# Two thirds of the tokens get all column chunks beside their GLA; attention's gates and output projections come in small pieces behind the heads

## The chip, the cores and the metric

One core of one Trainium2 chip. The metric is the device time of one launch in microseconds (us); lower is better. TensorE (PE) runs the matmuls and its weight loads (PEld), VectorE (DVE), ScalarE (ACT) and GpSimd (POOL) the rest; SyncE (SP) issues nearly all DMAs.

## What is computed

Two layers of a trunk over 256 context and 2048 latent tokens, 1024 wide, f32. A layer norms and modulates its input, projects it to columns for four mixers and their gates, mixes, and projects back:

```python
h = rms_norm(x, norm_w) * (1 + scale) + shift          # scale, shift, gate = ada(c)
p = split_proj(h @ w_in)                               # 12 chunks of 256 columns and a_lr
a = gla_mixer(...)       # A: gated linear attention, forward and backward over the tokens
b = fourier_mix(...)     # B: FFT over tokens and channels
c = swa_mixer(...)       # C: window attention, 4 heads, 2 key heads, sink logits, rope on q and k
d = na_mixer(...)        # D: 2-D neighbourhood attention, 4 heads, with a relative bias
y = concat([a * silu(a_g), b * silu(b_g), c * silu(c_g), d * silu(d_g)]) @ w_out
x = x + gate * y
```

Context tokens see context alone; latent tokens see both. Layer 1 needs no output for the context.

## The kernel before

**Tokens.** Nine subs of 256 tokens: sub 0 is the context, 1 to 8 the latents. Three groups: T1 = subs 0 to 2, T2 = 3 to 5, T3 = 6 to 8. The activations of a sub lie in SBUF as a pair of high and low f32r parts (`hh`, `hl`, tags of the pool `hp` with 3 buffers each, so one group at a time). Weights come in blocks of 256 columns, 1 MB in four DMAs, and are split in the same way (`load_w`, L204: ScalarE casts, VectorE and GpSimd subtract in turn; `whi`, `wlo` with 2 buffers). A product is three matmuls for each of 8 blocks of the contraction (`mm3`, L216). One chunk of one sub is 2 x 24 = 48 matmuls into one PSUM tile (`ps`, or `pso` in the output projection; pool `pp`, 2 buffers), called a block below.

**Chunks.** `project` (L277) ends a block by its kind: `cq`, `ckv`, `dk`, `dq` are normed (`normrope`, L367; cq and ckv with rope), transposed and stored; the gates `ag`, `bg`, `cg`, `dg` become silu by ScalarE and VectorE and are stored in `scr_g`; the others are stored as they are.

**Order.** The program is written in one sequence; a planner then orders each engine's instructions by its own model of times: whatever has its inputs and a free buffer, first by its place in the written sequence. `high_priority` moves what stands under it to the front of that order. Each engine then runs its list strictly in order.

**A layer** (`trunk`, L1198). For T1 and T2: `first_chunks` (L1157) norms h and projects av, lr, aqk, and stores h in DRAM (`scr_h`, L261); `mix_a` (L1167) loads GLA's inputs, then writes the chunks given as `between` (T1: bv, ckv, dk, dv; T2 those and dq), then `gla_fast` for each sub, then the ada blocks that it is given (`ada_block`, L158: VectorE reductions over weights from DRAM). In layer 0, ada(0, [1]) goes with T1 and ada(1, [0]) with T2. T3 has its kv chunks behind its GLA, then the guard, backward scan (`gla_bwd`) and FFT (`fnet`), then cq and dq. Layer 1 runs layer 0's output projection of T2 (`out_proj(0, [3])`, `[4, 5]`) behind T1's GLA.

**Attention** (`attention`, L1181; `pipeline`, L876). A list of items, one per head and query tile. The front of item i (L822) puts scores into the one PSUM tile `pse` (L830), reduces them with bias and sink on VectorE (L836, negative minimum kept in `am`) and takes the exponential on ScalarE (L844), the reciprocal of its sum on VectorE (L847). Behind items i-2 and i-3 stand the transposes (`ppt`, L862, and of the reciprocals, L866), their copies, the products with v (`py`, L922) and the output (L925). A neighbourhood head loads its bias (L1012, one buffer for each of two alternating heads, in three of four column groups). Phases as integers are neighbourhood row groups (16 items each), lists are window tiles (4 items each), None is the context's rows (8 items): 144 items in layer 0, 128 in layer 1; 64 in each are neighbourhood items over latents.

Between phases stand steps written as whole: `gate(T)` projects four gates of a group; `redo` (L1238) reloads a group's h from `scr_h` (`reload_h`, L264: load, cast, subtract) and projects cq (and dq); `out_proj` (L1088) loads y and g, multiplies (L1083, in place in y, one buffer), splits (`prep_mix`, L1073), then runs 4 blocks a sub, adding to x (L1107). In layer 0, T1's output projection stands behind all heads. All steps read in `ph` (L1247 to L1252).

Of the kernel before, what the change touches and what calls it, by code (L numbers as in the profile page):

```python
# [18 lines left out]
KB = 8  # L19
# [18 lines left out]
class Kern:  # L38
# [205 lines left out]
    def prep_h(self, L, s, save, xs=None):  # L244
# [4 lines left out]
        for t in range(2):  # L249
# [10 lines left out]
            if save:  # L260
                nc.sync.dma_start(self.sh[s][:, :, c], x)  # L261
        return hh, hl

    def reload_h(self, s):  # L264
        nc = self.nc
        hh = self.hp.tile([128, KB, SUB], F32R, tag="hh", name="hh2")
        hl = self.hp.tile([128, KB, SUB], F32R, tag="hl", name="hl2")
        for t in range(2):
            c = slice(t * 128, t * 128 + 128)
            x = self.xp.tile([128, KB, 128], F32, tag="xa", name="x2", bufs=3)  # L270
            nc.sync.dma_start(x, self.sh[s][:, :, c])
            nc.scalar.copy(hh[:, :, c], x)
            (nc.gpsimd if t else nc.vector).tensor_tensor(out=hl[:, :, c], in0=x, in1=hh[:, :, c], op=ALU.subtract)
        return hh, hl
# [798 lines left out]
    def prep_mix(self, L, s):  # L1073
        nc = self.nc
        hh = self.hp.tile([128, KB, SUB], F32R, tag="hh", name="mh")
        hl = self.hp.tile([128, KB, SUB], F32R, tag="hl", name="ml")
        for t in range(2):
            c = slice(t * 128, t * 128 + 128)
# [5 lines left out]
            nc.scalar.copy(hh[:, :, c], y)  # L1084
            (nc.gpsimd if t else nc.vector).tensor_tensor(out=hl[:, :, c], in0=y, in1=hh[:, :, c], op=ALU.subtract)  # L1085
        return hh, hl

    def out_proj(self, L, subs):  # L1088
        nc, a = self.nc, self.a
        with self.tc.high_priority():  # L1090
            mix = {s: self.prep_mix(L, s) for s in subs}
        ws = {}
        for j, s in self.order(range(4), subs):
            if j not in ws:
                with self.tc.high_priority():
                    ws[j] = self.load_w(a["w_out"][L, j])
            wh, wl = ws[j]
            st = 1 if s == 0 else 0
            hh, hl = mix[s]
            ps = self.pp.tile([128, 2, SUB], F32, tag="p", name="pso")  # L1100
            for b in range(2):
                c = slice(b * 128, b * 128 + 128)
                self.mm3(ps[:, b], lambda k: wh[:, k, c], lambda k: wl[:, k, c], lambda k: hh[:, k], lambda k: hl[:, k])
            x = self.ev.tile([128, 2, SUB], F32, tag="sq", name="xo")
            nc.sync.dma_start(x, self.xsrc[L][s][:, 2 * j:2 * j + 2])
            for b in range(2):
                nc.vector.scalar_tensor_tensor(out=x[:, b], in0=ps[:, b], scalar=self.mod[L, "gm"][:, 2 * j + b, st:st + 1], in1=x[:, b], op0=ALU.mult, op1=ALU.add)  # L1107
            nc.sync.dma_start(self.xdst[L][s][:, 2 * j:2 * j + 2], x)


    def scratch(self, L):
# [8 lines left out]
        self.sh = sc("h", [128, KB, SUB])  # L1120
# [36 lines left out]
    def first_chunks(self, L, subs, names, save=True, xs={}):  # L1157
        h = {}
        w = {nm: self.chunk_w(L, nm) for nm in names}
        for s in subs:  # L1160
            with self.tc.high_priority():
                h[s] = self.prep_h(L, s, save and not (L == 1 and s == 0), xs.get(s))
# [18 lines left out]
    def attention(self, L, *phases):  # L1181


        with self.tc.tile_pool(name=f"at{L}", bufs=2) as p:
            items, self.bias = [], {}
# [197 lines left out]
```

## Time and profile before

| what | us |
|---|---|
| median of 3 runs | 2922.6 (2921.6 to 2927.07) |
| the profiled execution | 2924.73 |
| its span, first to last instruction | 2922.9 |
| PE busy | 2702.4 |
| DVE busy | 1619.6 |
| ACT busy | 1066.4 |
| POOL busy | 865.5 |

The span is of one profiled execution, and the sums are made against that execution's time. PEclk is the clock granted to TensorE as a share of 2.4 GHz, a mean over a stretch in which it stands at 2.4 or at 1.2 GHz. Matmuls follow each other in a pipeline, so the mean duration of one is longer than its distance to the next. A wait line says which instruction's engine stood idle and what ended that.

### The profile page before, as it was taken

What the parts mean: (1) busy time and instruction counts of PE and PEld (TensorE: products, weight loads), DVE (VectorE), ACT (ScalarE), POOL (GpSimd) and SP (SyncE); (2) the same over time, 40 slices, a digit from 0 to 9 for tenths busy, and PEclk for the clock granted to TensorE, in tenths of its full rate; (3) what the DMA queues carried; (4) which work ended last, traced back from release to release, by engine and by line L of the source; (5) the groups of instructions that cost most, each with busy time, mean ns of one, the idle gap of its engine ahead of it and who ended that gap; (6) DMA issues with size and microseconds to landing.
All of it is one profiled execution on the core that took longest, in us unless ns stands there. A gap on an engine that the chain in (4) does not pass through costs nothing. (4 is left out here: it accounts for less than half of the span.)

```text
span 2922.9 us, 55816 instructions
## 1 busy us (share of the span) xinstructions
PE 2702.4 (92%) x21206; PEld 2404.3 (82%) x21206; DVE 1619.6 (55%) x3741; ACT 1066.4 (36%) x2344; POOL 865.5 (30%) x922
## 2 busy tenths in 40 slices
PE   5989879988999999999969899999889999999999
PEld 5989869977888778887869799889878888878789
DVE  7564774557465545645483554464583656455544
ACT  3343323323344434344224323334232544444332
POOL 3142322334231213212133333332362413121223
PEclk9999979999999999999979899999999999999999
DMA  8644544255765365453453565342465754556545
GB/s 286 203 123 148 183 127 129 87 165 161 188 175 155 119 176 159 135 169 119 138 184 125 177 199 157 100 129 87 128 184 165 207 150 138 156 159 192 154 140 187
DMA packets 476682, 458.01 MB, mean 157 GB/s; under 512 B 54763, under 2 KB 355565, under 8 KB 476013
## 3 DMA queue, kind: packets, MB, share of 16 engines
q1 hardware_dynamic: 472782, 440.66, 49.7%
q0 software_dynamic: 3616, 13.64, 1.9%
q8 instruction: 170, 2.79, 0.4%
q14 instruction: 114, 0.93, 0.1%
HBM read 339.56 MB, written 114.60 MB: 155 GB/s over the span
## 5 line engine op out<-in xcount | busy, mean ns | idle before, releaser
L220 PE MATMUL ps<-whi,hh 128*128 128x256 f32 x1968 | 588.6, 299 | 40.1 <-DVE nsq L376 21.7
L222 PE MATMUL ps<-whi,hl 128*128 128x256 f32 x1968 | 584.3, 297 | 8.7 <-DVE hl L259 8.5
L221 PE MATMUL ps<-wlo,hh 128*128 128x256 f32 x1968 | 582.6, 296 | 6.4 <-PEq L639 6.4
L213 POOL TENSOR_TENSOR wlo<-wraw,whi 128x512 fp32r<-128x512 f32 x208 | 304.8, 1478 | 580.0 <-ACT whi L212 520.7
L220 PEld LDWEIGHTS ps<-whi,hh 128*128 128x128 f32 x1968 | 394.1, 200 | 50.1 <-DVE nsq L376 20.8
L222 PEld LDWEIGHTS ps<-whi,hl 128*128 128x128 f32 x1968 | 393.7, 200 | 17.2 <-DVE hl L259 12.0
L221 PEld LDWEIGHTS ps<-wlo,hh 128*128 128x128 f32 x1968 | 394.7, 201 | 12.3 <-issue 9.2
L220 PE MATMUL ps<-hh,whi 128*128 128x256 f32 x1376 | 399.5, 290 | 1.9 <-DVE nsq L376 1.9
L222 PE MATMUL ps<-hh,wlo 128*128 128x256 f32 x1376 | 399.9, 291 | 0.0
L221 PE MATMUL ps<-hl,whi 128*128 128x256 f32 x1376 | 396.9, 288 | 0.0
L844 ACT ACTIVATE S<-S,am 128x641 f32<-128x641 f32 (+5 forms) x272 | 226.2, 832 | 358.9 <-DVE am L836 345.4
L220 PE MATMUL pso<-mh,whi 128*128 128x256 f32 x1088 | 318.3, 293 | 1.3 <-DVE xo L1107 1.3
L221 PE MATMUL pso<-ml,whi 128*128 128x256 f32 x1088 | 318.4, 293 | 0.0
L222 PE MATMUL pso<-mh,wlo 128*128 128x256 f32 x1088 | 317.3, 292 | 0.0
L212 ACT CAST whi<-wraw 128x512 fp32r<-128x512 f32 x416 | 230.5, 618 | 142.6 <-PE ps L221 43.2
L191 POOL TENSOR_TENSOR rs<-ms,mhalf 128x8 f32<-128x8 f32 (+2 forms) x140 | 174.2, 1246 | 351.1 <-DVE ms L189 339.9
L222 PEld LDWEIGHTS ps<-hh,wlo 128*128 128x128 f32 x1376 | 263.6, 192 | 11.3 <-issue 10.9
L213 DVE TENSOR_TENSOR wlo<-wraw,whi 128x512 fp32r<-128x512 f32 x208 | 200.7, 972 | 130.3 <-ACT whi L212 118.0
L220 PEld LDWEIGHTS ps<-hh,whi 128*128 128x128 f32 x1376 | 263.8, 192 | 10.1 <-issue 6.5
L221 PEld LDWEIGHTS ps<-hl,whi 128*128 128x128 f32 x1376 | 263.6, 192 | 8.3 <-issue 8.2
L830 PE MATMUL pse<-kst,q 64*128 64x256 f32 (+2 forms) x1184 | 245.2, 458 | 18.0 <-DVE am L836 15.6
L862 PE MATMUL ppt<-idn,S 128*128 128x128 f32 x1360 | 243.6, 284 | 12.9 <-DVE pt L872 4.9
(203 smaller groups left out, 4860.4 us busy)
## 6 DMA issues: line engine op xcount, KB each, us to landing
wraw<-w_in SPq DMA_DIRECT2D x288, 256.0 KB
wraw<-w_out SPq DMA_DIRECT2D x128, 256.0 KB
adaw<-ada_w SPq DMA_DIRECT2D x82, 256.0 KB
scr_g<-ev SPq DMA_DIRECT2D x68, 256.0 KB
g<-scr_g SPq DMA_DIRECT2D x34, 512.0 KB
y<-scr_y SPq DMA_DIRECT2D x34, 512.0 KB
bias<-nbias SPq DMA_DIRECT2D x48, 256.0 KB
scr_h<-x SPq DMA_DIRECT2D x22, 512.0 KB
```

What stands on the lines that cost most here:

```text
L191: nc.gpsimd.tensor_tensor(out=rs, in0=ms, in1=self.mhalf.to_broadcast([128, n]), op=ALU.pow)
L212: nc.scalar.copy(hi[:, k], raw)
L213: (nc.gpsimd if i % 4 else nc.vector).tensor_tensor(out=lo[:, k], in0=raw, in1=hi[:, k], op=ALU.subtract)
L220: nc.tensor.matmul(out, ah(k), bh(k), start=(k == 0), stop=False)
L221: nc.tensor.matmul(out, ah(k), bl(k), start=False, stop=False)
L222: nc.tensor.matmul(out, al(k), bh(k), start=False, stop=(k == KB - 1))
L830: nc.tensor.matmul(p[:, lo:hi], q[r], k, start=True, stop=True, tile_position=(64 * o, 0))
L844: nc.scalar.activation(out=S[:, 0:w], in_=S[:, 0:w], func=AF.Exp, scale=-1.0, bias=m[:, 0:1], accum_out=m[:, 1:2])
L862: nc.tensor.transpose(p[:, i], S[:, (c0 + i) * 128:(c0 + i + 1) * 128], self.idn)
```

## The change

- T1 and T2 get all their chunks as `between` of `mix_a`: kv, then cq, dq and the four gates (`rest`). h is no longer stored or reloaded; `reload_h` and `redo` are gone.
- In layer 0, ada(1, [0]) moves from T2's `mix_a` to T3's.
- Attention gets its side work in pieces, each behind a given item, where it was whole steps between phases. In layer 0: T3's 12 gate blocks behind items 4 to 54; T3's output projection from item 57, its six half loads two items apart, then 12 blocks to item 102; T1's from item 105, half loads one item apart, then 12 blocks to item 142. In layer 1: gates 4 to 54, T3 from 57 to 87, T1 (two subs) from 89 to 126, and after attention `out_proj` of [3, 4] and [5].
- `prep_mix` writes the product into g (3 buffers) in place of y (1 buffer); each half's product stands one step behind its load, and in attention it is pinned behind the VectorE instruction written before it.
- A piece asks for its own weight block and the next.

```diff
-    def reload_h(self, s):
...
-    def prep_mix(self, L, s):
...
-            nc.vector.tensor_tensor(out=y, in0=y, in1=g, op=ALU.mult)
...
+    def prep_mix(self, L, subs, late=False):
...
+        def product(s, c):
+            g, y = got.pop(0)
+            hh, hl = mix[s]
+            ins = nc.vector.tensor_tensor(out=g, in0=y, in1=g, op=ALU.mult)
+            if late:
+                self.tc.keep_in_program_order(ins)
+            nc.scalar.copy(hh[:, :, c], g)
+            (nc.gpsimd if c.start else nc.vector).tensor_tensor(out=hl[:, :, c], in0=g, in1=hh[:, :, c], op=ALU.subtract)
+        halves = [(s, slice(t * 128, t * 128 + 128)) for s in subs for t in range(2)]
+
+        def step(k):
+            if k > 0:
+                product(*halves[k - 1])
+            if k < len(halves):
+                load(*halves[k])
...
+    def pieces(self, order, load, run):
+
+        blocks = list(dict.fromkeys(j for j, _ in order))
+        ws = {}
+
+        def piece(j, s):
+            for x in blocks[blocks.index(j):][:2]:
+                if x not in ws:
+                    with self.tc.high_priority():
+                        ws[x] = load(x)
+            run(j, s, ws[j])
+        return [lambda j=j, s=s: piece(j, s) for j, s in order]
...
+            def give(lo, hi, fs):
+                for k, f in enumerate(fs):
+                    behind.setdefault(lo + k * (hi - lo) // max(len(fs) - 1, 1), []).append(f)
+
+            def out(lo, step, hi, subs):
+                made = []
+                n = 2 * len(subs)
+
+                def prep(k):
+                    if k == 0:
+                        mix, steps = self.prep_mix(L, subs, True)
+                        made.extend((steps, self.out_pieces(L, subs, mix)))
+                    made[0][k]()
+                give(lo, lo + step * n, [lambda k=k: prep(k) for k in range(n + 1)])
+                give(lo + step * n + 1, hi, [lambda k=k: made[1][k]() for k in range(4 * len(subs))])
...
-            self.mix_a(L, T1, (0, [1]) if L == 0 else (1, [1]), lambda: self.chunks(L, T1, kv, h))
+            qs = ["dq", "cq"]
+
+            def rest(subs, h):
+
+                self.chunks(L, subs, kv + qs + gates[:2], h)
+                self.chunks(L, subs, gates[2:], h)
+            self.mix_a(L, T1, (L, [1]), lambda: rest(T1, h))
...
-            self.mix_a(L, T2, (1, [0]) if L == 0 else None, lambda: self.chunks(L, T2, kv + ["dq"], h))
-            h = self.first_chunks(L, T3, first, False)
-            self.mix_a(L, T3)
+            self.mix_a(L, T2, None, lambda: rest(T2, h))
+            h = self.first_chunks(L, T3, first)
+            self.mix_a(L, T3, (1, [0]) if L == 0 else None)
             self.chunks(L, T3, kv, h)
...
+            gate = self.pieces(self.order(gates, T3), lambda nm: self.chunk_w(L, nm), lambda nm, s, w: self.project(L, nm, s, h[s], w))
             if L == 0:
-                ph += [b(self.out_proj, L, T3), b(redo, T2, ["cq"]), 1, [4, 5, 6, 7, 8, 9], gate(T2), f(self.out_proj, L, T1)]
+                self.attention(L, [3, 2, [10, 11, 12, 13, 14, 15], 0, [-2, -1, 0, 1, 2, 3], None, 1, [4, 5, 6, 7, 8, 9]],
+                               [(4, 54, gate), (57, 2, 102, T3), (105, 1, 142, T1)])
             else:
...
+                self.attention(L, [3, 2, [10, 11, 12, 13, 14, 15], 0, [0, 1, 2, 3], 1, [4, 5], [6, 7], [8, 9]],
+                               [(4, 54, gate), (57, 2, 87, T3), (89, 2, 126, T1)])
+                self.out_proj(L, [3, 4])
+                self.out_proj(L, [5])
```

## Rows read from the trace of the kernel before

**Rows 1.** Page, part 1: engine busy us (share) xinstructions.

```profile
PE 2702.4 (92%) x21206; PEld 2404.3 (82%) x21206; DVE 1619.6 (55%) x3741; ACT 1066.4 (36%) x2344; POOL 865.5 (30%) x922
```

**Rows 2.** Busy by stretch: length, engines busy (instructions), PEclk, DMA share, GB/s.

```profile
63.00:305.00 242.00, 228.93 (x1790) 219.21 (x1790) 139.85 (x317) 86.50 (x179) 73.13 (x65) 0.99 0.52 163
305.00:451.00 146.00, 121.65 (x790) 108.56 (x791) 110.30 (x273) 47.74 (x113) 45.61 (x35) 0.84 0.47 142
451.00:600.00 149.00, 146.50 (x1158) 139.28 (x1157) 70.61 (x171) 57.87 (x131) 42.02 (x38) 0.99 0.36 114
757.00:1457.00 700.00, 680.82 (x5757) 574.46 (x5756) 365.95 (x863) 279.75 (x644) 158.40 (x236) 0.99 0.52 153
1457.00:1550.00 93.00, 60.54 (x400) 57.22 (x399) 67.13 (x146) 22.69 (x37) 32.86 (x29) 0.80 0.62 191
1550.00:1750.00 200.00, 184.42 (x1396) 177.51 (x1395) 98.11 (x188) 71.59 (x144) 70.58 (x58) 0.94 0.53 165
1750.00:1920.00 170.00, 159.78 (x1202) 151.95 (x1201) 82.63 (x180) 63.66 (x137) 58.51 (x49) 0.93 0.40 121
2237.00:2816.00 579.00, 566.32 (x4833) 466.94 (x4835) 317.08 (x741) 252.10 (x575) 144.82 (x212) 0.99 0.58 166
```

**Rows 3.** Busy by stretch: 40 us of output projection alone, layer 1's end.

```profile
2870.00:2910.00 40.00, 40.00 (x335) 40.00 (x335) 6.40 (x15) 1.00 0.67 212
```

**Rows 4.** Busy by stretch, tile ps alone: PE first, both attentions.

```profile
757.00:1457.00 700.00, 256.44 (x1803) 227.47 (x1801) 25.96 (x38) 22.47 (x38) 0.99 0.52 153
2237.00:2816.00 579.00, 214.50 (x1488) 187.24 (x1488) 21.65 (x32) 18.45 (x31) 0.99 0.58 166
```

**Rows 5.** Busy by stretch, tile pso alone: PE first, both attentions.

```profile
757.00:1457.00 700.00, 165.11 (x1148) 145.65 (x1149) 20.14 (x46) 0.99 0.52 153
2237.00:2816.00 579.00, 110.28 (x744) 95.28 (x744) 13.06 (x30) 0.99 0.58 166
```

**Rows 6.** Waits, 305 to 451: who <- for whom: us, times, longest.

```profile
PE ps L220 <- DVE nsq L376: 14.0, 4, 9.4
...
DVE adaj L167 <- DMA adaw<-ada_w: 17.3, 6, 5.0
```

**Rows 7.** Groups, 305 to 451: VectorE's ada reductions | busy, mean ns | idle.

```profile
L167 DVE CUSTOM_DVE_ANT_0 adaj<-adaw,csb,ada 128x512 f32<-128x512 f32 x32 | 27.1, 846 | 6.0 <-DMA adaw<-ada_w 5.6
L167 DVE CUSTOM_DVE_ANT_0 adaj<-adaw,csb 128x512 f32<-128x512 f32 x32 | 22.6, 705 | 12.1 <-DMA adaw<-ada_w 11.7
```

**Rows 8.** Timeline, TensorE at 1040: start us, us, engine, line, op, tiles.

```profile
1040.30 0.91 PE L830 MATMUL pse<-kst,q 64*128 64x384 f32 x4
1041.14 0.44 PE L862 MATMUL ppt<-idn,S 128*128 128x128 f32 x2
1041.41 0.27 PE L866 MATMUL ppt<-idn,rd 128*128 128x128 f32 x1
1041.52 0.49 PE L862 MATMUL ppt<-idn,S 128*128 128x128 f32 x3
1042.25 0.91 PE L830 MATMUL pse<-kst,q 64*128 64x384 f32 x4 [0.23 <-DVE am L836]
```

**Rows 9.** Timeline, VectorE at 1041, the same heads.

```profile
1041.36 0.82 DVE L836 CUSTOM_DVE_ANT_0 S<-pse,bias 128x640 f32<-128x640 f32 x1
...
1043.18 0.16 DVE L847 RECIPROCAL rc<-am 128x1 f32<-128x1 f32 x1 [0.52 <-ACT S L844]
```

**Rows 10.** Timeline at 769: one bias load and the reduction behind it.

```profile
769.22 0.55 SPq L1012 DMA_DIRECT2D bias<-nbias  x1
...
774.14 0.82 DVE L836 CUSTOM_DVE_ANT_0 S<-pse,bias 128x640 f32<-128x640 f32 x1 [0.71 <-DMA bias<-nbias]
```

**Rows 11.** Waits, 757 to 1457, of TensorE and of VectorE.

```profile
PE pse L830 <- DVE am L836: 10.8, 7, 5.1
...
DVE y L1083 <- DMA y<-scr_y: 34.5, 10, 5.4
```

**Rows 12.** Page, part 6: DMA issues xcount, KB each.

```profile
scr_h<-x SPq DMA_DIRECT2D x22, 512.0 KB
```

More of the change, by code (lines that the diff above doesn't have):

```diff
@@ L1070, in na_ctx_rows, with load @@
                 for a in ((hp, t, i) for hp in range(2) for t in range(2) for i in range(2))]
-    def prep_mix(self, L, s):
+    def prep_mix(self, L, subs, late=False):
         nc = self.nc
[L1075 to L1078, printed above, removed]
+        mix = {s: [self.hp.tile([128, KB, SUB], F32R, tag=n, name=m) for n, m in (("hh", "mh"), ("hl", "ml"))] for s in subs}
+        got = []
+        def load(s, c):
             g = self.xp.tile([128, KB, 128], F32, tag="xa", name="g", bufs=3)
@@ L1092, in out_proj @@
-        ws = {}
[L1093 to L1108, printed above, removed]
+            for f in steps:
+                f()
@@ new lines, in out_proj, with out_pieces @@
+        for f in self.out_pieces(L, subs, mix):
+            f()
+    def out_pieces(self, L, subs, mix):
+        return self.pieces(self.order(range(4), subs), lambda j: self.load_w(self.a["w_out"][L, j]), lambda j, s, w: self.out_block(L, j, s, mix[s], w))
+    def pieces(self, order, load, run):
+        blocks = list(dict.fromkeys(j for j, _ in order))
+        ws = {}
+        def piece(j, s):
[5 more added lines that the diff above has]
+        return [lambda j=j, s=s: piece(j, s) for j, s in order]
@@ L1161, in first_chunks @@
             with self.tc.high_priority():
-                h[s] = self.prep_h(L, s, save and not (L == 1 and s == 0), xs.get(s))
+                h[s] = self.prep_h(L, s, xs.get(s))
             for nm in names:
@@ L1179, in mix_b, with attention @@
             self.fnet(L, p, ctx)
-    def attention(self, L, *phases):
+    def attention(self, L, phases, spread):
         with self.tc.tile_pool(name=f"at{L}", bufs=2) as p:
-            items, self.bias = [], {}
+            items, self.bias, behind = [], {}, {}
+            def give(lo, hi, fs):
[11 more added lines that the diff above has]
+                give(lo + step * n + 1, hi, [lambda k=k: made[1][k]() for k in range(4 * len(subs))])
+            for sp in spread:
+                (out if len(sp) == 4 else give)(*sp)
             for ph in phases:
@@ L1190, in attention, with wrap, last @@
                     items += self.na(L, p, ph)
-                elif isinstance(ph, tuple):
-                    run, nop = lambda f=ph[1]: f(), lambda *r: None
-                    items.append((None, run, nop) if ph[0] == "before" else (None, nop, lambda r, x, f=ph[1]: x == 2 and f()))
-                elif ph:
+                else:
                     items += self.swa(L, p, ph)
-            self.pipeline(items)
+            def wrap(i, item):
+                def last(r, x):
+                    item[2](r, x)
+                    if x == 2:
+                        for f in behind.pop(i, []):
+                            f()
+                return item[0], item[1], last
+            self.pipeline([wrap(i, it) for i, it in enumerate(items)])
+            assert not behind
     def trunk(self):
```

56 lines of the change are left out of this document (21 added, 35 removed).

## The prediction

> **What bounds the kernel now.** I read the page's first part, then the busy time by stage, then waits and timelines inside the stages. TensorE is busy 2702.4 us of 2922.9, VectorE 1619.6, ScalarE and GpSimd less [rows 1]: the end is set by TensorE's work and by its holes. That work does not change here, since the change only moves blocks. So the question is what the holes cost, stage by stage.
>
> I price a stage as its idle time (length less PE busy) plus what the lower clock costs, (1 - PEclk) x PE busy: a mean of 0.84 is 2.4 GHz for about two thirds of a stage and 1.2 GHz for the rest. From the rows by stage [rows 2]: layer 0, tokens T1 (63 to 305 us) 13.1 + 2.3 = 15; T2 (305 to 451) 24.4 + 19.5 = 44; T3's GLA (451 to 600) 4; attention (757 to 1457) 19.2 + 6.8 = 26. Boundary to layer 1 (1457 to 1550) 32.5 + 12.1 = 45. Layer 1: T1 with layer 0's late output projections (1550 to 1750) 27; T2 (1750 to 1920) 21; attention (2237 to 2816) 12.7 + 5.7 = 18. Together 200 us of 2922.9. The holes sit beside the GLA and at the boundary; attention, 1279 us long, has few. A change that takes work out of attention and lays it beside GLA moves filler from a place where it is used to a place where it lacks.
>
> **The change part by part.**
>
> *Size of what moves.* A dense stretch of output projection issues 335 matmuls in 40 us, 0.119 us each [rows 3]; a block (one chunk, one sub) is 48 of them, 5.73 us. In layer 0, T1's cq, dq and gates (6 chunks x 3 subs) and T2's cq and gates (5 x 3) go from attention to GLA: 33 blocks, 189 us. In layer 1 sub 0 needs none: 12 + 15 = 27 blocks, 155 us. By itself this adds to one stage what it takes from another: 0.
>
> *T2 of layer 0.* The 44 us has one named cause beside the lack of filler: TensorE waited 14.0 us, once 9.4, for a projection's PSUM that VectorE had not read [rows 6], while VectorE worked through ada(1, [0]): 64 reductions, 27.1 + 22.6 = 49.7 us [rows 7], and stood 17.3 us more waiting for their weights [rows 6]. The change puts 15 more blocks there (cq and the four gates; dq was there) and takes the ada away. T1's stage, which had 12 column blocks beside its GLA, loses 15 of 242 us, 6%. At that rate T2 loses 9 to 10: **gain 34**, bounds 0 (GLA queues behind the chunks and runs bare afterwards) and 40.
>
> *The ada in T3.* The same 49.7 us now lies with T3's GLA, ahead of T3's remaining chunks and of the backward scan and FFT. VectorE is busy 70.6 of 149 us there [rows 2]; with 49.7 and 17.3 of waiting it comes to 138 of 149. PE has filler there, yet its PSUM is freed by the same VectorE. Bounds: 4 as now, 44 as in T2. I take 20, nearer to now since the stage has filler throughout: **cost 16**.
>
> With the blocks go their weights and ends: 11 chunk loads a layer, 44 DMAs of 256 KB on SP's queue behind GLA's small loads and stores, their casts on ScalarE, half the subtractions each on VectorE and GpSimd, and the norm and rope of cq and dq. T2's stage has room for its part: without the ada's 49.7, VectorE is busy 61 of 146 us, ScalarE 48, GpSimd 46, and DMA is at 0.47 [rows 2]. Cost 0; without that room it would be D's price, below.
>
> *Layer 1, T1 and T2.* T1 keeps ada(1, [1]), T2 has none, before and after; 27 blocks arrive. At T1's 6% they would lose 13 and 11 in place of 27 and 21: **gain 24**, bounds 0 and 40.
>
> *Boundary.* Last out-projection of layer 0, store, load, norm, projection of layer 1: a chain. T1's projections now run among the last heads instead of alone behind them, so the first two subs end a little before the attention's drain. **Gain 5**, bounds -5 and 17 (three blocks' cover).
>
> *Attention with less filler.* Layer 0's attention holds 1803 ps and 1148 pso matmuls [rows 4, 5], 2951 x 0.119 = 352 us; the other 680.8 - 352 = 328 us are the 144 heads' own, 2.28 us each. Layer 1: 2232 matmuls, 266 us, leaving 300 us for 128 heads, 2.34 us. So a head had 20.5 filler matmuls (17.4 in layer 1). 33 x 48 = 1584 of the 1803 leave: 219 + 1148 = 1367, 9.5 a head. (45 blocks are traced for this stretch, 2160 matmuls, and only 1803 lie in it: 357 ran before the first head although they stand behind 56 heads in the program. The order is greedy, filler is pulled as far ahead as its inputs allow.) In layer 1, 1488 - 1296 = 192 and 20 output blocks, 960: 9.0 a head.
>
> If pieces are pulled ahead and each head that has any takes as many as now, 1367 / 20.5 = 67 heads are fed and 77 are bare; in layer 1, 66 fed and 62 bare: 139. Price of a bare head: two stand in the trace. From one score matmul to the next 1.95 us, transposes alone between them [rows 8]; VectorE's round from reduction over ScalarE's exponential to reciprocal 1.98 us [rows 9]. Both are under the 2.3 us of a head's own work, so a bare head of the window attention idles little: 0 to 0.3, I take 0.15. A neighbourhood head needs its bias in one buffer for every second head: issue at 769.22, reduction started at 774.14, having waited for it [rows 10], so 4.9 + 0.8 + 0.1 of reduction = 5.8 to 5.9 for two heads, 2.95 each, 0.64 over its own work. 128 of the 272 heads are of that kind: 65 x 0.64 + 74 x 0.15 = 53 us. Other bound: evenly spread, 3.4 us of PE work a head is over 2.95 and nothing is lost.
>
> *The product y x g.* Now VectorE waited 34.5 us for y in layer 0's attention, and PE 10.8 us for reductions behind it [rows 11]. The pinned product comes two heads after its load (4.6 us bare), which covers most of waits of 3.45 us on average; for T1 of layer 0 one head after, six times, where VectorE still stands some 1.2 us (3.45 - 2.3) with the next heads' reductions and copies queued behind it. y is free after the product instead of after the cast and the subtraction. I take 5 us on PE, bounds 0 and 15.
>
> Attention after: 53 + 5 + 12.5 of clock as now = 70 against 44 now: **cost 26**, bounds a gain of 20 (nothing bare, no waits) and a loss of 100 (below).
>
> *Removed.* 22 stores of h and 22 loads of 512 KB each [rows 12], with cast and subtraction of every load. ScalarE is busy 279.8 and VectorE 366.0 of attention's 700 us, DMA at 0.52 [rows 2], so they cost TensorE nothing and give back nothing; if that cover were gone they would be a gain. *The tail of layer 1*: out_proj of subs 3 to 5 keeps 12 blocks, 69 us, to cover their own loads; 0. Weights are loaded as often as before.
>
> **Sum.** 34 - 16 + 24 + 5 - 26 = 21 us. The profiled execution took 2924.7 us (span 2922.9, the rest around it), 0.1% over the median of 2922.6. 2924.7 - 21 = 2903.7, and 2901.6 against the median; I say 2903.
>
> **The rivals.**
>
> *A, forecast: 2903, chance 0.44.* GLA is covered, half the heads are bare at full clock.
>
> *B, slower: the clock falls in the bare heads: 2961, chance 0.22.* The lower level follows idle stretches: 0.84 where TensorE idled 17% (T2), 0.80 where it idled 35% (boundary), 0.99 in attention, where it idled 3% [rows 2]. Bare heads idle up to a fifth. 139 x 2.31 = 321 us of work; at a clock of 0.82, 58 us are lost: 2903 + 58. It decides from a mean of 0.93 in those heads, where 21 us is gone. Against it: a bare head's hole is 0.15 to 0.64 us, where T2's longest wait was 9.4 [rows 6]. The Trainium skill, "TensorE: Matmul & The Clock Gate", section "A second HAM failure mode: psum-queue depth-cycling", says that micro-idling between groups of matmuls is enough to make the clock swing between its levels; by that rule B would come, while the trace's 0.99 beside 3% idle neither agrees nor disagrees, as no run so far has bare heads in a row.
>
> *C, better: the pieces stay where they are traced: 2850, chance 0.18.* That is the change doing what its words say. The 53 us fall away: 2903 - 53. Against it: the 357 matmuls pulled ahead.
>
> *D, the ada hurts T3 as it did T2: 2927, chance 0.16.* T3 loses 44 instead of 20: 2903 + 24. For it: 138 of 149 us of VectorE.
>
> **How the numbers follow.** Faster or slower by over 0.2% is about what a measurement of this kernel can tell, so the bounds are 2916.8 and 2928.4. A gives faster 0.36, same 0.06, slower 0.02; B slower 0.21, same 0.01; C faster 0.18; D faster 0.03, same 0.05, slower 0.08. Sums: faster 0.57, same 0.12, slower 0.31. The range 2850 to 2965 takes in A, D, half of C and most of B.
>
> **What would show it.** T2 of layer 0: clock over 0.95 and idle under 10 us; else the first gain fails. The ada's 64 reductions between T3's GLA and the FFT, with PE's waits on nsq there: D. In both attentions: count of heads with no ps or pso between two score matmuls (139 by A, few by C), their period (2.3 to 3.0), and PEclk (0.99 by A, under 0.93 by B). Attention of layer 0 should last some 491 us of work and 35 of holes, about 525 in place of 700; layer 1's stretch 437 + 35. Waits of VectorE on y should fall from 34.5 us to under 15. The prediction is wrong if attention gets no shorter than its blocks' 189 us explain less 60, or if GLA's stages keep their clock of 0.84 and 0.93.

## The result and the profile after

The changed kernel takes 2884.72 us in the median (2877.26 to 2889.81) where the kernel before takes 2922.74 (2921.6 to 2927.07): a ratio of 0.9865, 95% interval 0.9839 to 0.9891, faster by 38 us. Predicted were 2903 us, range 2850 to 2965. The profiled execution of the changed kernel took 2889.81 us, its span 2887.7, so the two traces are 34.9 us apart.

Page of the changed kernel, part 1, to be set beside [rows 1]:

```profile
PE 2686.7 (93%) x21206; PEld 2382.0 (82%) x21206; DVE 1614.2 (56%) x3730; ACT 1037.1 (36%) x2322; POOL 833.3 (29%) x911
```

As many matmuls run, 21206, so the gain lies in holes and clock. The next rows are the changed kernel's busy time by stretch, columns as in [rows 2]. In their order: layer 0's GLA of T1 and T2, T3's GLA, backward scan and FFT, attention, the boundary; layer 1's T1 with the late output projections, T2, scan and FFT, attention.

```profile
63.00:605.00 542.00, 529.87 (x4214) 512.53 (x4215) 287.14 (x602) 186.50 (x385) 178.72 (x145) 0.99 0.39 123
605.00:757.00 152.00, 144.99 (x1134) 137.35 (x1134) 104.79 (x274) 52.47 (x125) 37.12 (x27) 0.98 0.51 158
757.00:933.00 176.00, 151.57 (x975) 132.82 (x974) 105.71 (x259) 41.60 (x94) 70.18 (x61) 0.91 0.55 163
933.00:1448.00 515.00, 482.97 (x4004) 369.88 (x4005) 296.84 (x757) 222.18 (x545) 103.16 (x208) 0.97 0.56 153
1448.00:1520.00 72.00, 69.58 (x562) 67.77 (x562) 56.09 (x118) 26.40 (x45) 16.93 (x16) 0.95 0.79 248
1520.00:1745.00 225.00, 219.07 (x1772) 212.94 (x1771) 127.93 (x238) 81.14 (x169) 95.64 (x68) 0.99 0.54 165
1745.00:2012.00 267.00, 258.24 (x2060) 249.95 (x2059) 133.01 (x279) 92.14 (x189) 96.03 (x82) 0.97 0.38 119
2155.00:2331.00 176.00, 148.39 (x966) 131.78 (x966) 100.94 (x252) 41.20 (x91) 68.14 (x57) 0.90 0.52 156
2331.00:2817.00 486.00, 446.77 (x3724) 340.76 (x3725) 267.53 (x655) 205.65 (x498) 89.26 (x180) 0.97 0.59 162
```

Priced as in the prediction (length less PE busy, plus (1 - PEclk) x PE busy):

| stage | before, us lost | after | gain | predicted |
|---|---|---|---|---|
| layer 0, T1 and T2 | 15 + 44 | 12.1 + 5.3 = 17 | 42 | 34 |
| layer 0, T3's GLA with the ada | 4 | 7.0 + 2.9 = 10 | -6 | -16 |
| boundary | 45 | 2.4 + 3.5 = 6 | 39 | 5 |
| layer 1, T1 and T2 | 27 + 21 | 8 + 17 = 25 | 23 | 24 |
| both attentions | 26 + 18 | 46.5 + 52.6 = 99 | -55 | -26 |

That sums to a gain of 43, against 21 predicted. Of the stages not listed here, scan and FFT lose 38 + 42 us where they lost 34 + 35 (600 to 757 and 2078 to 2237 before), and T3's GLA in layer 1 loses next to nothing where it lost 6. With them the sum is within 1 or 2 us of the 35 by which the traces differ, as near as a clock of two digits can tell. Two terms were mis-sized by about 30 us each, on opposite sides: the boundary and attention. The experiments are about these two, about the ada, and about which part of the change carries the gain.

Waits of VectorE in the changed kernel, first in layer 0's attention (933 to 1448), then in layer 1's (2331 to 2817); us in total, times, longest:

```profile
DVE S L822 <- DMA bias<-nbias: 30.2, 11, 8.2
...
DVE g L1075 <- DMA y<-scr_y: 15.2, 8, 3.7
...
DVE g L1075 <- DMA y<-scr_y: 29.6, 8, 9.0
...
DVE S L822 <- DMA bias<-nbias: 22.4, 9, 6.8
```

Waits of TensorE in the same two stretches, in the same order:

```profile
PE pse L816 <- DVE am L822: 24.4, 38, 3.0
...
PE pse L816 <- DVE am L822: 25.3, 30, 6.2
```

TensorE's wait for the reductions has grown from 10.8 us [rows 11] to 24.4 in layer 0, and VectorE stands now for two loads, the bias and y. Both are loads that a head, or a product written between heads, finds not yet landed. The sign that the prediction gave, waits for y under 15 us where layer 0 had 34.5, was just missed there (15.2); in layer 1 they fell from 39.8 to 29.6.

### The profile page after: what moved, and what is told of

Its sections match the earlier page's. It is cut to its first block, busy times and chain, and to the rows that moved or that the text cites. A ratio compares the mean times of both kernels' runs of the same rounds, so it can differ in the third digit from the quotient of the medians.

```text
span 2887.7 us, 55904 instructions
## 1 busy us (share of the span) xinstructions
PE 2686.7 (93%) x21206; PEld 2382.0 (82%) x21206; DVE 1614.2 (56%) x3730; ACT 1037.1 (36%) x2322; POOL 833.3 (29%) x911
## 5 line engine op out<-in xcount | busy, mean ns | idle before, releaser
L220 PE MATMUL ps<-whi,hh 128*128 128x256 f32 x1968 | 574.9, 292 | 6.4 <-DVE nsq L362 3.9
L221 PE MATMUL ps<-wlo,hh 128*128 128x256 f32 x1968 | 571.4, 290 | 6.4 <-PEq L625 6.4
L222 PE MATMUL ps<-whi,hl 128*128 128x256 f32 x1968 | 570.0, 290 | 3.0 <-issue 2.1
L220 PEld LDWEIGHTS ps<-whi,hh 128*128 128x128 f32 x1968 | 384.7, 195 | 13.3 <-DVE nsq L362 4.4
L221 PEld LDWEIGHTS ps<-wlo,hh 128*128 128x128 f32 x1968 | 384.6, 195 | 9.6 <-issue 7.3
L222 PEld LDWEIGHTS ps<-whi,hl 128*128 128x128 f32 x1968 | 384.4, 195 | 6.0 <-issue 2.3
L816 PE MATMUL pse<-kst,q 64*128 64x256 f32 (+2 forms) x1184 | 253.1, 465 | 53.3 <-DVE am L822 49.6
L213 DVE TENSOR_TENSOR wlo<-wraw,whi 128x512 fp32r<-128x512 f32 x208 | 207.0, 1001 | 146.6 <-ACT whi L212 139.5
L848 PE MATMUL ppt<-idn,S 128*128 128x128 f32 x1360 | 227.0, 287 | 8.4 <-ACT pt L856 4.2
```

The source lines that it names most:

```text
L213: (nc.gpsimd if i % 4 else nc.vector).tensor_tensor(out=lo[:, k], in0=raw, in1=hi[:, k], op=ALU.subtract)
L220: nc.tensor.matmul(out, ah(k), bh(k), start=(k == 0), stop=False)
L221: nc.tensor.matmul(out, ah(k), bl(k), start=False, stop=False)
L222: nc.tensor.matmul(out, al(k), bh(k), start=False, stop=(k == KB - 1))
L816: nc.tensor.matmul(p[:, lo:hi], q[r], k, start=True, stop=True, tile_position=(64 * o, 0))
L848: nc.tensor.transpose(p[:, i], S[:, (c0 + i) * 128:(c0 + i + 1) * 128], self.idn)
```

## The experiments

All times are medians, each beside runs of the kernel before on the same chip; the last column is the 95% interval of the ratio to before. The ratio can differ by 0.1 or 0.2% from the quotient of the two medians, so small differences are judged by the interval.

| kernel | us | before there | difference | ratio | interval |
|---|---|---|---|---|---|
| changed kernel | 2884.7 | 2922.7 | -38.0 | 0.9865 | 0.9839 to 0.9891 |
| e1_before_ada_t3 | 2920.0 | 2922.1 | -2.1 | 1.0002 | 0.9989 to 1.0016 |
| e2_columns | 2948.4 | 2922.1 | +26.4 | 1.0087 | 1.0060 to 1.0113 |
| e3_columns_ada | 2927.4 | 2922.1 | +5.4 | 1.0018 | 0.9995 to 1.0042 |
| e4_after_ada_t2 | 2898.0 | 2922.1 | -24.1 | 0.9927 | 0.9898 to 0.9956 |
| e5_t1_behind | 2889.8 | 2920.3 | -30.4 | 0.9880 | 0.9853 to 0.9907 |
| e6_gates_pinned | 2986.1 | 2920.3 | +65.8 | 1.0214 | 1.0177 to 1.0251 |
| e7_not_late | 2923.5 | 2920.3 | +3.2 | 1.0010 | 0.9994 to 1.0027 |
| e8_bias_once | 2860.5 | 2920.3 | -59.8 | 0.9780 | 0.9757 to 0.9804 |
| e9_bias_ahead | 2864.5 | 2917.2 | -52.7 | 0.9814 | 0.9788 to 0.9840 |
| e10_y_ahead | 2870.8 | 2917.2 | -46.3 | 0.9842 | 0.9824 to 0.9861 |
| e11_bias_steps3 | 2838.4 | 2917.2 | -78.8 | 0.9733 | 0.9714 to 0.9752 |
| e12_before_bias_ahead | 2920.0 | 2922.5 | -2.4 | 0.9991 | 0.9975 to 1.0008 |

The second table puts the attentions side by side: loss by the formula above from the rows by stretch of each trace, and bare heads counted in the trace (score matmuls of one head up to those of the next with no ps or pso between).

| kernel | loss, layer 0 + layer 1 | bare heads | mean period of one, us |
|---|---|---|---|
| before | 26 + 18 | 4 + 1 | |
| changed kernel | 46.5 + 53 | 71 + 73 | 2.75, 2.65 |
| e3_columns_ada | 64 + 71 | 67 + 58 | 2.93, 3.00 |
| e7_not_late | 60 + 72 | 72 + 60 | 2.78, 2.99 |
| e6_gates_pinned | 49 + 64 | 63 + 63 | 2.81, 2.78 |
| e9_bias_ahead | 34 + 44 | 71 + 73 | 2.62, 2.50 |
| e10_y_ahead | 36 + 43.5 | 71 + 71 | 2.58, 2.57 |
| e11_bias_steps3 | 26 + 18 | 79 + 76 | 2.52, 2.49 |

### The parts alone: e1, e2, e3, e4

e1 is the kernel before with only the ada moved:

```diff
-            self.mix_a(L, T2, (1, [0]) if L == 0 else None, lambda: self.chunks(L, T2, kv + ["dq"], h))
+            self.mix_a(L, T2, None, lambda: self.chunks(L, T2, kv + ["dq"], h))
...
-            self.mix_a(L, T3)
+            self.mix_a(L, T3, (1, [0]) if L == 0 else None)
```

> The kernel before with one edit: ada(1, [0]) goes with T3's GLA and not with T2's. Theory 1 (T2's hole is lack of filler, the ada only part of it): T2 of layer 0 keeps a hole of 20 to 30 us out of 44, T3 loses about 9 as in the changed kernel in place of 4; time 2905 to 2912. Theory 2 (the ada's work on VectorE made the hole): T2's loss falls to 10 and the time to about 2890, that is most of the change's gain by this line alone.

Measured: no change, where both theories saw a gain. Its rows by stretch, T1 and T2, then T3's GLA:

```profile
63.00:430.00 367.00, 347.93 (x2641) 329.66 (x2642) 210.80 (x472) 138.63 (x297) 119.82 (x105) 0.96 0.46 142
430.00:567.00 137.00, 130.46 (x967) 120.51 (x966) 113.17 (x285) 49.62 (x118) 39.86 (x32) 0.95 0.56 176
```

T1 and T2 lose 19.1 + 13.9 = 33 us in place of 59, T3's GLA 6.5 + 6.5 = 13 in place of 4. So in the trace these stages do about what was expected. Scan and FFT (567 to 748) lose 41 us in place of 34, and 26 - 9 - 8 is the 9.6 us by which this one profiled execution is shorter than that of before. But the two executions lie toward opposite ends of their kernels' spread (2915.1, where e1's ten runs span 2914.2 to 2927.2, and 2924.7, where 19 runs of before span 2907.9 to 2928.7). The medians are 2.1 us apart, with an interval of some 4 us on either side of no change. So whether anything of the 9.6 us is real stays open.

e2 is the kernel before with all column chunks beside GLA and no h stored or reloaded; e3 is e2 with the ada at T3. Output projections and T3's gates stay whole steps between the phases.

```diff
-            self.mix_a(L, T1, (0, [1]) if L == 0 else (1, [1]), lambda: self.chunks(L, T1, kv, h))
+            qs = ["dq", "cq"]
+
+            def rest(subs, h):
+                self.chunks(L, subs, kv + qs + gates[:2], h)
+                self.chunks(L, subs, gates[2:], h)
+            self.mix_a(L, T1, (0, [1]) if L == 0 else (1, [1]), lambda: rest(T1, h))
...
-            ph = [3, 2, [10, 11, 12, 13, 14, 15], gate(T3), b(redo, T1, ["cq", "dq"]), 0, ctx[0] + [0, 1, 2, 3], *ctx[1:], gate(T1)]
+            ph = [3, 2, [10, 11, 12, 13, 14, 15], gate(T3), 0, ctx[0] + [0, 1, 2, 3], *ctx[1:]]
```

> The kernel before with one part of the change: T1 and T2 get all their column chunks beside GLA, h is neither stored nor reloaded; the ada stays with T2, and attention's gates of T3 and output projections stay whole steps as before. Theory 1 (the gain is filler moved to where it lacks; the hole at the layer boundary closes because less filler stands ahead of T1's output projection): about 2895, the boundary's hole of 30 us idle under 10. Theory 2 (the small pieces close the boundary's hole and keep attention fed): 2915 to 2930, boundary as before.

> As the run before, and the ada with T3. It differs from the changed kernel in attention's pieces alone. Theory 1: within 10 us of the changed kernel, 2880 to 2895. Theory 2 (the pieces matter): 2910 or more. The difference to the run before is the price of the ada's place with filler there: 0 to 10 us by theory 1.

Measured: e2 is 26 us slower than before, e3 5 us slower with an interval that holds no change. The time of e2 lies outside both of its theories, that of e3 in the second, by which the pieces matter. Moving the columns is by itself no gain: what GLA's stages and the boundary win, attention gives back. One sign of e2's first theory did come: its boundary closes. In the 73 us from the end of its heads (1477 to 1550) TensorE is busy 70.0 at a mean clock of 0.95, and no matmul of an output projection (pso) is left there, though T1's still stands whole behind the heads. Both attentions of e3:

```profile
924.00:1457.00 533.00, 493.79 (x4028) 378.16 (x4029) 294.50 (x742) 219.90 (x540) 94.22 (x202) 0.95 0.52 147
2351.00:2857.00 506.00, 457.94 (x3761) 349.19 (x3761) 272.25 (x655) 208.78 (x499) 91.41 (x180) 0.95 0.55 156
```

Loss 39.2 + 24.7 and 48.1 + 22.9, together 135 us against 44 before. The rest of the change (pieces, pinned product, product in g, weight blocks asked for one ahead) is worth 43 us (from +5.4 to -38.0).

e4 is the changed kernel with the ada back in T2, the reverse of e1's edit.

> The changed kernel with one line undone: ada(1, [0]) back with T2. Theory 1: T2 is filled now, so the ada costs there what it cost in T3 (5 us) or little more: 2885 to 2895. Theory 2 (the ada makes the hole whatever lies there): T2 loses 30 or more again, 2910.

Measured: 13 us slower than the changed kernel, between the two theories; the move is worth 21 us between e2 and e3. So the ada's place costs where GLA has all the filler beside it, and no cost was measured in the kernel before. In the changed kernel T3 shows why it is cheap there. Waits of VectorE, then of TensorE, 605 to 757 us:

```profile
DVE adaj L167 <- DMA adaw<-ada_w: 14.2, 6, 5.6
```

```profile
PE pz L477 <- DMA lrt<-scr_lr: 6.5, 1, 6.5
```

VectorE stands for the ada's weights as it did in T2 [rows 6], but no wait of TensorE on a reduction (nsq) comes of it; its one large wait there is for another load.

### The pinned product: e7

```diff
-                        mix, steps = self.prep_mix(L, subs, True)
+                        mix, steps = self.prep_mix(L, subs)
```

> The changed kernel, with the product of y and g not pinned in VectorE's order. Theory 1: the planner places it too early, VectorE waits 80 to 100 us in all for y in place of 45, and heads behind it are late: 5 to 15 us slower, 2890 to 2900. Theory 2 (those waits are hidden behind filler): within 3 us of 2885.

Measured: 2923.5 us, no faster than before and far beyond the first theory's 2890 to 2900. One pin is worth 41 us (from -38.0 to +3.2), more than the whole of the gain, and pieces without it end where e3's whole steps do. The reverse, whole steps whose product is kept behind its load, was not tested. The attentions of e7:

```profile
930.00:1463.00 533.00, 492.61 (x4035) 375.24 (x4035) 301.37 (x768) 223.92 (x546) 104.09 (x210) 0.96 0.53 151
2345.00:2847.00 502.00, 452.08 (x3717) 342.46 (x3718) 272.21 (x655) 208.02 (x498) 90.98 (x180) 0.95 0.56 157
```

Loss 60 + 72 where the changed kernel has 46.5 + 53: 33 us more, nearly all of the 34 between the two profiled executions. The timeline of e7 shows how. The lines are SP's issue of a load of y, then VectorE, then TensorE:

```profile
1090.38 0.56 SPq L1068 DMA_DIRECT2D y<-scr_y  x1
...
1095.17 1.23 DVE L1075 TENSOR_TENSOR g<-y,g 128x1024 f32<-128x1024 f32 x1 [4.53 <-DMA y<-scr_y]
1096.31 0.55 DVE L858 COPY pt<-ppt 128x384 f32<-128x384 f32 x1
...
1096.92 0.47 PE L848 MATMUL ppt<-idn,S 128*128 128x128 f32 x1 [4.67 <-DVE pt L858]
```

VectorE reaches the product 0.3 us after its load is issued (1095.17 - 4.53 = 1090.64) and stands 4.53 us. The copy of the next head's transposes (pt) is queued behind it, so TensorE stands 4.67 us. Without the pin the planner puts the product directly behind its load, and the step of two heads is lost: over layer 0's twelve products the lead from issue to VectorE's arrival is 0.3 to 3.5 us; in the changed kernel T3's six have 4.5 us and more, T1's 2.0 to 7.8. TensorE's idle time from VectorE's arrival at a product to 1.5 us after the product's end, summed over the 22 products that lie behind heads, is 46 us in e7 and 22 in the changed kernel; elsewhere in the attentions e7 idles 5 us less. The other 14 of the 33 us are clock: 19.7 + 22.6 us in e7's attentions, 14.5 + 13.4 in the changed kernel's.

### Where the filler lies: e5 and e6

e5 writes T1's output projection of layer 0 as one step behind all heads, as the kernel before does:

```diff
-                               [(4, 54, gate), (57, 2, 102, T3), (105, 1, 142, T1)])
+                               [(4, 54, gate), (57, 2, 102, T3)])
+                self.out_proj(L, T1)
```

> The changed kernel, with T1's output projection of layer 0 whole and behind the last head, as out_proj, in place of pieces between heads 105 and 142. Theory 1 (the order in which filler is pulled decides, not where it is written): its blocks are pulled among the same heads, boundary idle stays under 10 us, time within 8 us of 2885. Theory 2 (the pieces' place hid the boundary's chain): the boundary's 30 us idle and its low clock return, 2910 to 2920.

Measured: 2889.8 us, ratio 0.9880, as the changed kernel within the intervals. The rows by stretch for tile pso alone say where that projection ran. The kernel before, from its last head (1421) to the end of the projection:

```profile
1421.00:1457.00 36.00, 31.64 (x250) 30.39 (x251) 4.38 (x10) 1.00 0.58 184
```

The changed kernel, last 27 us of the heads, then the boundary:

```profile
1421.00:1448.00 27.00, 13.00 (x88) 11.13 (x88) 1.73 (x4) 1.00 0.43 135
1448.00:1520.00 72.00, 0.00 (x0) 0.00 (x0) 0.00 (x0) 0.95 0.79 248
```

e5, the same two stretches:

```profile
1417.00:1444.00 27.00, 6.98 (x50) 6.21 (x50) 1.72 (x4) 1.00 0.55 176
1444.00:1507.00 63.00, 0.00 (x0) 0.00 (x0) 0.00 (x0) 1.00 0.72 228
```

Before, 250 matmuls of it were left when the heads ended, with T2's cq and gates ahead of them as filler. With those gone the projection is through before the last head wherever it is written, and layer 1's chain of load and norm starts early. That is the boundary's 39 us; e2 above, where the moved columns alone close the boundary, shows the same.

e6 pins the first matmul of each of T3's gate blocks to its place in the program, so that the gates really lie behind heads 4 to 54:

```diff
...
-            nc.tensor.matmul(out, ah(k), bh(k), start=(k == 0), stop=False)
+            ins = nc.tensor.matmul(out, ah(k), bh(k), start=(k == 0), stop=False)
+            if pin and k == 0:
+                self.tc.keep_in_program_order(ins)
...
```

> The changed kernel, with the first matmul of each of T3's 12 gate blocks held behind the TensorE instruction written before it, so that the blocks stay behind heads 4 to 54 in both layers and can't be pulled ahead of the first head. Theory 1 (144 bare heads cost idle time and some clock, some 38 us idle in all): the heads 8 to 54 are no longer bare, attention loses 15 to 25 us less in both layers together, the stretch before it loses little: 2865 to 2875. Theory 2 (the blocks pulled ahead fill holes of the backward scan and FFT): those stages lose as much as attention gains, 2880 to 2890.

Measured: 101 us slower than the changed kernel, against both theories. Rows by stretch of e6: scan and FFT, attention, in layer 0 and then in layer 1.

```profile
757.00:913.00 156.00, 99.70 (x485) 74.16 (x483) 94.20 (x245) 31.80 (x75) 63.54 (x57) 0.82 0.53 156
913.00:1492.00 579.00, 546.73 (x4481) 426.87 (x4481) 305.92 (x768) 234.22 (x561) 111.11 (x212) 0.97 0.51 144
...
2200.00:2359.00 159.00, 104.78 (x519) 81.04 (x518) 90.33 (x239) 32.34 (x74) 63.97 (x53) 0.80 0.49 146
2359.00:2912.00 553.00, 514.55 (x4190) 401.03 (x4190) 274.88 (x667) 218.12 (x515) 96.74 (x184) 0.95 0.55 150
```

In layer 0, scan and FFT run 485 matmuls where the changed kernel runs 975, and end only 20 us sooner (156 for 176): 490 matmuls, 58 us at 0.119 us each [rows 3], had filled holes there. They lose 56.3 + 17.9 = 74 us in place of 38; in layer 1 75 in place of 42. Attention takes the blocks at full price, 64 and 67 us longer. Its bare heads become 63 + 63, hardly fewer, and its loss is 49 + 64. So the gates earn their place in scan and FFT, into which the planner pulls them, and not behind the heads.

### The two loads: e8, e9, e10, e11, e12

e8 loads the bias for the first column group only:

```diff
-                nc.sync.dma_start(pool_st["b", i][:, a0:512], self.a["nbias"][L, (0, 1, 1, 2)[rg], CG_TYPE[cg]][:, 2 * hp + i, 0:nloc])
+                if cg == 0:
+                    nc.sync.dma_start(pool_st["b", i][:, a0:512], self.a["nbias"][L, (0, 1, 1, 2)[rg], CG_TYPE[cg]][:, 2 * hp + i, 0:nloc])
```

> The changed kernel, with the neighbourhood bias loaded for the first of the column groups alone, 32 of 96 loads; the other groups use that bias, so part of the computation is left out. Theory 1 (bare neighbourhood heads idle for their bias): VectorE's waits of 30 and 22 us for bias fall under 10, TensorE loses 10 to 20 us less: 2865 to 2875. Theory 2 (the waits lie beside other work): within 4 us of 2885.

Measured: 2860.5 us, 22 to 24 us faster than the changed kernel and a little beyond the first theory; VectorE's waits for the bias fell to 9.5 us in layer 0 and 13.9 in layer 1. e9 keeps every load, with two tiles for each of the two heads and each load issued a column group ahead:

```diff
+        def bias(i, n):
+            if ("b", i, n % 2) not in pool_st:
+                b = pool_st["b", i, n % 2] = pool.tile([128, 768], F32, name=f"bias{i}{n % 2}", bufs=1)
...
-                if ("b", i) not in pool_st:
-                    b = pool_st["b", i] = pool.tile([128, 768], F32, name=f"bias{i}", bufs=1)
...
+                for x in ([0, 1] if n == 0 else [n + 1] if n < 5 else []):
+                    bias(i, x)
```

> The changed kernel with two bias tiles for each of the two heads instead of one, and each load issued one column group ahead; everything is computed. Theory 1: the one tile is what makes DVE wait (30.2 and 22.4 us for the bias in the two attention stretches), since a load can start only when the tile's last reader is through. Then this keeps most of what loading the bias once gave (24 us): 2860 to 2870 us. Rival: it was the number of transfers, not the tile; there are as many here, so 2880 to 2890 us, with the same waits for the bias.

e10 gives y a second tile and issues its load two steps ahead of the product:

```diff
+            if late and c.start:
+                y = late.tile([128, KB, 128], F32, tag="yx", name="y", bufs=1)
...
-            if k > 0:
-                product(*halves[k - 1])
+            if k >= far:
+                product(*halves[k - far])
```

> The changed kernel with a second tile for the attention output y, so that each load is issued two steps (four heads) ahead of its product instead of one. Theory 1: PE stands 26 us beside the 24 products that lie behind heads (10 us in layer 0, 16 in layer 1), because DVE waits there for y and holds the next head's scores back, and the clock falls behind the longest of these; with the load ahead most of that goes: 2855 to 2870 us. Rival: the wait is not the load's lead but its place on the queue of SP, or DVE is late by as much in its other work, so that another wait takes its place: 2878 to 2888 us.

e11 is e9 with three heads in place of two between a load of y and its product, for T3 in both layers and T1 in layer 1:

```diff
...
-                               [(4, 54, gate), (57, 2, 102, T3), (105, 1, 142, T1)])
+                               [(4, 54, gate), (57, 3, 102, T3), (105, 1, 142, T1)])
...
-                               [(4, 54, gate), (57, 2, 87, T3), (89, 2, 126, T1)])
+                               [(4, 54, gate), (57, 3, 87, T3), (89, 3, 126, T1)])
```

> The changed kernel with two bias tiles for each head, loaded a column group ahead, and three heads instead of two between a load of y and its product (the output blocks follow in fewer heads). Theory 1: the two waits add up, and a third head is about half of what the two-step lead gives: 2845 to 2860 us. Rival: the blocks lie closer together, more heads are left bare, and the gain of the bias alone is all there is: 2862 to 2872 us.

Measured beside each other on one chip: e9 -52.7, e10 -46.3, e11 -78.8 us against before, where the changed kernel, beside its own runs of before, has -38.0. e9 keeps 15 of the 22 us of e8. Waits of VectorE for the bias in layer 0's attention fall from 30.2 us to this, in e9:

```profile
DVE S L822 <- DMA bias<-nbias: 6.3, 1, 6.3
```

So the one tile, and the late issue that it forces, made the wait, and the rival falls; the edit changes tile and issue together. e10 comes out just past its theory's slow end by the median, 14 us under the changed kernel, but only 8 by the differences to before, and the two intervals overlap. TensorE's idle time beside the 22 products (the expectation counted 24) falls from 22 to 7 us, and the clock's part from 28 to 14, yet part returns elsewhere. VectorE in e10's layer 0 and then layer 1, the waits for the bias (30.2 and 22.4 in the changed kernel) and for y:

```profile
DVE S L822 <- DMA bias<-nbias: 33.0, 13, 6.3
...
DVE g L1078 <- DMA y<-scr_y: 1.6, 2, 1.2
...
DVE S L822 <- DMA bias<-nbias: 27.1, 13, 6.0
...
DVE g L1078 <- DMA y<-scr_y: 21.6, 4, 8.9
```

The 21.6 us that are left in layer 1 are not at the pinned products: they belong to the first four products of the late projections, `out_proj` of [3, 4], which have no pin.

e11 gains 26 us more than e9, beyond its theory; it is the fastest kernel here, 46 us under the changed kernel by the medians. Its attentions:

```profile
928.00:1427.00 499.00, 477.72 (x4006) 365.86 (x4005) 296.67 (x755) 221.48 (x544) 103.89 (x208) 0.99 0.57 159
2313.00:2763.00 450.00, 432.18 (x3701) 329.49 (x3702) 271.06 (x655) 204.99 (x498) 93.76 (x180) 1.00 0.64 175
```

The loss is 26 + 18 us, as in the kernel before, with 155 bare heads. In layer 1 it was 52.6 us in the changed kernel and 44 in e9; of the 26 from e9 to e11, 13 are clock. VectorE's waits for y hardly fall in sum (32.6 us in e9, 29.9 in e11, layer 1). What falls is what they hold up: TensorE idles 3.3 us beside the first ten products in place of 11.8, and 3.2 beside the six of the late projections ([3, 4] and [5]) in place of 11.5. At the first of these six VectorE arrives 4.7 us before the load is issued in e9, and 1.8 us after it in e11. Why, when their steps were not touched, was not tested.

e12 is the kernel before with e9's edit.

> The kernel before with the same two bias tiles, loaded one column group ahead. Theory 1: a late load costs PE time only behind a head without other matmuls; before has 5 such heads where the changed kernel has 144, and DVE waits 8.6 and 5.8 us for the bias: no change, 2914 to 2925 us. Rival: the wait delays the heads whatever stands behind them, and the edit is worth about as much here as in the changed kernel (20 us): 2895 to 2905 us.

Measured: 2920.0 us, ratio 0.9991, no change; waits of VectorE for the bias in its 757 to 1457 were 7.8 us, and 8.6 in the kernel before. With filler behind nearly every head the same single tile costs nothing that can be measured; with half the heads bare it costs some 15 us (by medians 20; the intervals of e9 and of the changed kernel just meet). The two kernels differ in more than their bare heads, so that these are the reason is argued, not tested alone.

## Why the prediction was right, and where it was not

Direction and range held, and so did the outline of forecast A: GLA is covered, half the heads are bare, and the clock holds in them. Its steps:

- **T2 and T1 of layer 0, gain 34: right.** 42 us, clock 0.99, idle 12 us over both groups. The forecast took its 6% of the stages' lengths without the blocks that arrive; with them its losses would have been 4 to 6 us higher in each group, here and in layer 1. Measured were 3% of the 542 us here and 5% of the 492 us in layer 1.
- **The ada in T3, cost 16: too high, 6.** The term assumed that VectorE at 138 of 149 us would hold up PSUM; VectorE is busy 104.8 and waits 14.2 for the ada's weights, 119 of 152 us, and TensorE waited for no reduction (nsq) there. Rival D falls. Taken alone (e1) the move gave nothing; beside full filler (e4, e2 to e3) 13 to 21 us.
- **Layer 1, T1 and T2, gain 24: right,** 23 us.
- **Boundary, gain 5, bounds -5 and 17: mis-sized, 39.** The step saw that projections would run among the last heads, but counted only three blocks of cover. What it missed is the queue ahead: T1's output projection was late because T2's blocks stood before it, and e5 and e2 show it done with the heads even when written behind them.
- **Attention, cost 26, bounds -20 and 100: mis-sized, 55.** It lasted 515 and 486 us, where 525 and 472 were forecast. The count was right (139 bare heads predicted, 144 traced, though 87 of them neighbourhood heads where 65 were counted) and so was the greedy order that gives it; rival C falls, since all but 97 of the gates' matmuls run before the first head of layer 0. The price of an undisturbed bare head was near, if high. Score matmuls of the neighbourhood heads in the changed kernel, timeline of TensorE:

```profile
1020.53 0.93 PE L816 MATMUL pse<-kst,q 64*128 64x384 f32 x6
...
1022.53 0.93 PE L816 MATMUL pse<-kst,q 64*128 64x384 f32 x6 [0.15 <-DVE am L822]
...
1025.65 0.93 PE L816 MATMUL pse<-kst,q 64*128 64x384 f32 x6
...
1027.65 0.93 PE L816 MATMUL pse<-kst,q 64*128 64x384 f32 x6 [0.16 <-DVE am L822]
```

  2.00 + 3.12 us for a pair, 2.56 each, where 2.95 was taken. Over all bare neighbourhood heads, late loads included, the mean is 2.88 us in layer 0 and 2.73 in layer 1; bare window heads ran 2.42 and 2.53, where 2.43 and 2.49 were taken. Of the 71 us that TensorE idles in both attentions, 40 lie away from the products y x g, 19 of these where a reduction waits for its bias; 53 were forecast. So the bare heads as such did not make attention dearer than forecast.
- **The product y x g inside that, 5 us, bounds 0 and 15: the step that failed.** A lead of two heads, 4.6 us, was taken to cover a load because VectorE's mean wait was 3.45 us. But that wait is only what was left when VectorE had reached the product. From issue to product the loads took 4.3 to 6.9 us in the attentions of the kernel before, and up to 12.4 in the changed kernel. Its timeline, SP's issue, VectorE's product and next reduction, TensorE's next scores:

```profile
2533.14 0.55 SPq L1068 DMA_DIRECT2D y<-scr_y  x1
...
2545.51 1.23 DVE L1075 TENSOR_TENSOR g<-y,g 128x1024 f32<-128x1024 f32 x1 [5.72 <-DMA y<-scr_y]
2546.65 0.74 DVE L822 CUSTOM_DVE_ANT_0 S<-pse,cmask,sink 128x512 f32<-128x512 f32 x1
...
2547.46 1.22 PE L816 MATMUL pse<-kst,q 64*128 64x256 f32 x4 [6.20 <-DVE am L822]
```

  The lead was 6.7 us (arrival at 2539.8), the load took 12.4, TensorE stood 6.20. Such holes cost 22 us beside 22 products, and the clock 28 us where 12.5 was kept from before. By the same measure TensorE idled 27 us beside the 25 products in the attentions of the kernel before, so what was to shrink to 5 us hardly shrank. The pin's worth (e7, 41 us) was not priced at all: the prediction named it but counted its two heads as given.
- **The tail of layer 1, 0: mis-sized.** `out_proj` of [3, 4] has no pin, and four of its products are pulled among the last heads. SP's issue and VectorE's product for the first:

```profile
2740.95 0.54 SPq L1068 DMA_DIRECT2D y<-scr_y  x1
...
2745.62 1.23 DVE L1075 TENSOR_TENSOR g<-y,g 128x1024 f32<-128x1024 f32 x1 [9.02 <-DMA y<-scr_y]
```

  VectorE reached it at 2736.6, 4.3 us before the load was issued. These four make 19.5 of the 29.6 us of VectorE's waits for y in layer 1, and TensorE idles 10 us beside them. With that, attention's miss is accounted for: 13 us less in bare heads, 17 more beside the pinned products, 10 beside these, 15 of clock.
- **Rival B, the clock falls in bare heads: it did not.** Both attentions have a mean of 0.97, where B wanted under 0.93. Rows by stretch of the changed kernel: 80 us with bare heads in a row, then the ten us ahead of the hole above and the seven behind it.

```profile
1000.00:1080.00 80.00, 75.13 (x688) 50.70 (x687) 53.87 (x144) 43.24 (x112) 9.29 (x40) 1.00 0.45 124
...
2531.00:2541.00 10.00, 10.00 (x85) 7.99 (x85) 6.82 (x16) 4.59 (x11) 2.51 (x7) 1.00 0.94 219
2547.00:2554.00 7.00, 6.54 (x42) 5.65 (x42) 2.34 (x8) 2.78 (x7) 2.72 (x3) 0.56 0.60 172
```

  TensorE idles 4.9 of the 80 us, in 19 bits of at most 0.66 us, and stays at 2.4 GHz; behind the one hole of 6.20 us the mean is 0.56. Shorter single holes could have it fall too: over the 7 us behind a hole of 1.98 us (1115 to 1122) the mean is 0.76, over the 7 us behind one of 2.33 us (2366 to 2373) it is 1.00. All 11 stretches at 1.2 GHz in the two attentions begin in a single hole of 1.4 to 6.2 us or within 2 us of its end. So the clock's part of the loss goes with single holes, not with bare heads as such. The rule cited for B from the Trainium skill ("TensorE: Matmul & The Clock Gate", section "A second HAM failure mode: psum-queue depth-cycling") does not carry over to idling of this size; the trace disagrees with it here.
- **Removed stores and reloads, 0:** not tried alone.

So the sum came near by luck: two errors cancel, +34 at the boundary and -29 in attention, beside 18 us from the first two terms. The forecast's time was 18 us too long.

## What to carry to other kernels

Filler that is taken out of a stage also takes away the cover of every load in it that is only just in time, so before such a move, list those loads with the time from issue to use, lead and wait together, and set the lead by the longest; here a second bias tile was worth nothing measurable in the kernel before and some 15 us in the changed one. An instruction that waits for a load in an in-order engine's list costs by what stands behind it: where its place in that list decides, pin it and check in the timeline how far behind its load it really lies. And ask of each piece of filler which holes it fills now: e6 held the gates exactly where the change's title puts them and lost 101 us.

## What the runs showed of the hardware that was not expected

- Loads of 512 KB of y took from under 5 us (issue 1090.38 to the product at 1095.17, in e7) to 12.4 us (2533.14 to 2545.51, in the changed kernel, behind a stretch with a DMA share of 0.94 and 219 GB/s). A lead of 6.7 us, ample for most of them, was 5.7 us short there.
- The granted clock stayed at 1.00 through 80 us with 6% of idle time in bits of at most 0.66 us, and had a mean of 0.56 over the 7 us behind one hole of 6.20 us.
